# FFN down projection of two token passes by a seven-product scheme, on one core

## The chip, the core and the metric

The kernel runs on one core of a Trainium2 chip. The metric is the device time of one execution in microseconds. Engines are named as in the profile: PE is the matrix engine (PEld its weight loads), DVE the vector engine, ACT the scalar engine, POOL GpSimd, SP the engine that issues most transfers.

## What is computed

One layer of a transformer-like trunk: a gated mixer beside a cross-attention into 256 memory tokens, a projection with a normalised residual, and then a gated feed-forward network (FFN) with another normalised residual. D is 1024, there are 2048 tokens, and the FFN is 2816 wide.

```python
x = layer_norm(ALPHA * x + branch @ w_o, ln1_g, ln1_b)
x = layer_norm(ALPHA * x + swiglu_ffn(x, ffn_w_in, ffn_w_down), ln2_g, ln2_b)
# swiglu_ffn:
h = x @ w_in
(jax.nn.silu(h[..., :D_FF]) * h[..., D_FF:]) @ w_down
```

Matrices are stored transposed on the chip: features lie on the 128 partitions, tokens along the free axis. So x has 8 feature tiles, the FFN's inner width has 22 width tiles, and the output 8 output tiles.

## The kernel before

Every operand of a matmul is an fp32 matrix cut in a high and a low part (`split`, L71: ACT writes the rounded high part, L73, and DVE the rest, L74). A product of two split matrices takes three matmuls (`PASSES`: high by high, high by low, low by high).

After the mixer (to about 740 us of the span) the FFN runs in three token passes of 688, 680 and 680 tokens (`Pass`, `FPASSES`; their tiles carry the numbers 0, 1 and 2). A pass goes through its 22 width tiles in five blocks (`FBLOCKS`: 5, 4, 4, 4, 5). In a block come first the up projections (`up`, one for each width tile f), then the down projection of the block (`down`).

`up` works by seven products in place of eight already: the two halves of the tokens, the two halves of the inner dimension and the two matrices of the gate make 2x2 blocks, and the products run in the order 1, 6, 2, 5, 7, 3, 4 (12 matmuls each), into four PSUM banks. Between them DVE and ACT read the banks (`stages`). The weight combinations of products 3, 5, 6 and 7 are made in the first pass and kept in DRAM (`keep`, `ready`, L90). At the end the gated tile is split into `g`.

`down` takes each output tile m in turn: the weights of the block's nb width tiles are fetched (`weights`, tile `r_d`) and split (`w_d`), then 2 x nb x 3 matmuls of 340 tokens (344 in the first pass) fill two banks, and DVE adds each bank to the residual tile `fa` (L447 in the first block, L450 after). The fetch stands one output tile ahead of its matmuls. In the last block of a pass `done` also prepares the next pass's operands (`ffn.load`); in the last block of the third pass the columns are cut in 424 and 256.

The normalisation of a finished pass (`norm_steps`) runs between the products of the next pass's first five up projections; its last step stores `fa` (L460), and `residual` (L424) then loads the next pass's `fa` from `x1d` into the same buffers.

Tiles come from rings: raw weights `raw` has 4 buffers, split weights `wsp` 5, so that a tile waits until the one four (five) before it is read. A scheduler fixes the order of each engine's instructions when the program is built; PE keeps the order of the code. Each engine, and SP's queue, works through its own list in order, so that an instruction that waits holds up all behind it.

## Time and profile before

| | |
|---|---|
| time, median of 3 runs | 2175.59 us (2174.63 to 2178.59) |
| profiled execution: time / span | 2175.97 us / 2174.2 us |
| PE busy | 2111.3 us, 97% of the span |
| DVE busy | 1484.8 us, 68% |
| ACT busy | 874.4 us, 40% |
| POOL busy | 329.0 us, 15% |
| mean granted clock of PE | 0.993 |
| first pass, second, third (span's time) | 740 to 1231, 1231 to 1690, 1690 to 2174 us |

Busy times are of an engine's own instructions; a share is of the whole span, over stages that differ. In groups of instructions the columns are: line, engine, operation, output and inputs, shape and count, then busy time and mean duration in ns, then the idle time of the engine ahead of them and what ended it. In a timeline the columns are start, duration, instruction and count, and idle time with its releaser.

### The profile page before, as it was taken

The numbers are of one execution on the slowest core, as the hardware profiler recorded it, in microseconds if no ns is written. First come the engines' busy times: TensorE is split into PE (matmuls) and PEld (weight loads), VectorE is DVE, ScalarE is ACT, GpSimd is POOL, SyncE is SP. The second block draws the span as 40 slices with busy tenths as digits, with TensorE's granted clock in tenths as the row PEclk, the third lists the DMA queues.
The fourth block names the chain that finished last, engine by engine and source line by source line (L and its number), as shares of the span: only waits on it lengthen the run. The fifth ranks groups of instructions, "written<-read, shape, count | busy, mean of one in ns | idle before, by whom it ended". The sixth has DMA issues, their size and how long they took to land.

```text
span 2174.2 us, 34544 instructions
## 1 busy us (share of the span) xinstructions
PE 2111.3 (97%) x13130; PEld 2003.1 (92%) x13130; DVE 1484.8 (68%) x2702; ACT 874.4 (40%) x1710; POOL 329.0 (15%) x254
## 2 busy tenths in 40 slices
PE   9999999999999989999999999999999999999997
PEld 7888788788888879999999999999999999999996
DVE  7986796798789795767767874544548754454457
ACT  5553653564474452433434452222224342222234
POOL 1412321331322450000000320000002300000003
PEclk9999999999999999999999999999999999999998
DMA  6233314234333555545545565454454666445453
GB/s 214 78 110 124 117 64 160 98 107 143 129 97 111 174 201 191 208 161 178 196 158 204 192 229 194 156 194 150 160 197 147 222 220 204 154 148 198 150 181 99
DMA packets 126982, 348.83 MB, mean 160 GB/s; under 512 B 12640, under 2 KB 22880, under 8 KB 126816
## 3 DMA queue, kind: packets, MB, share of 16 engines
q1 hardware_dynamic: 113664, 299.41, 41.6%
q10 hardware_dynamic: 12672, 46.14, 5.4%
q8 instruction: 103, 1.69, 0.3%
q0 software_dynamic: 480, 1.07, 0.2%
q14 instruction: 63, 0.52, 0.1%
HBM read 283.66 MB, written 62.91 MB: 159 GB/s over the span
## 4 chain that ended last, share of the span: by engine, by line
PE 70%; DVE 17%; DMA 5%; issue 4%; ACT 3%; POOL 2%; ACTq 0%; DVEq 0%; SPq 0%; POOLq 0%
PE h L60 37%; PE d L60 19%; PE v L60 5%; PE u L60 3%; PE y L60 2%; DMA r_x<-in_xT 2%; DVE x L74 2%; DVE w_o L74 1%; DMA r_f<-x1d 1%; DVE w_u L74 1%; DVE z L567 1%; POOL s_a L233 1%; ACT p L610 1%; DVE w L74 1%; DVE w_d L74 1%
## 5 line engine op out<-in xcount | busy, mean ns | idle before, releaser
L60 PE MATMUL h<-x,w 128*128 128x340 f32 (+1 forms) x5544 | 878.6, 320 | 10.0 <-ACT m L405 3.3
L60 PEld LDWEIGHTS h<-x,w 128*128 128x128 f32 x5544 | 868.7, 188 | 16.0 <-ACT m L405 5.2
L60 PE MATMUL d<-g,w_d 128*128 128x340 f32 (+3 forms) x3168 | 504.7, 320 | 7.1 <-DVE w_d L74 4.2
L60 PEld LDWEIGHTS d<-g,w_d 128*128 128x128 f32 x3168 | 497.5, 189 | 11.4 <-DVE w_d L74 5.9
L73 ACT CAST w<-r_u 128x512 fp32r<-128x512 f32 x198 | 121.6, 619 | 260.1 <-PE h L60 163.0
L60 PE MATMUL y<-br,w_o 128*128 128x512 f32 x960 | 224.4, 395 | 0.0
L60 PEld LDWEIGHTS y<-br,w_o 128*128 128x128 f32 x960 | 180.4, 188 | 42.1
L60 PE MATMUL v<-w_v,x 128*128 128x512 f32 x768 | 187.8, 401 | 6.5 <-ACT w_v L73 4.8
L450 DVE TENSOR_TENSOR fa<-fa,d 128x340 f32<-128x340 f32 (+3 forms) x192 | 97.2, 507 | 132.4 <-PE d L60 132.4
L74 DVE TENSOR_TENSOR w<-r_u,w 128x512 fp32r<-128x512 f32 x198 | 141.1, 715 | 66.4 <-ACT w L73 56.6
L60 PEld LDWEIGHTS v<-w_v,x 128*128 128x128 f32 x768 | 143.5, 190 | 42.0 <-ACT w_v L73 4.8
L73 ACT CAST w_d<-r_d 128x512 fp32r<-128x512 f32 (+2 forms) x184 | 95.4, 521 | 202.5 <-PE d L60 145.8
L74 DVE TENSOR_TENSOR w_d<-r_d,w_d 128x512 fp32r<-128x512 f32 (+2 forms) x184 | 108.8, 597 | 48.4 <-ACT w_d L73 45.7
L369 POOL TENSOR_TENSOR t<-r_f,r_f 128x340 f32<-128x340 f32 (+1 forms) x12 | 13.9, 1161 | 813.0 <-DMA r_f<-x1d 406.4
L73 ACT CAST g<-c 128x340 fp32r<-128x340 f32 (+1 forms) x132 | 63.1, 478 | 109.7 <-DVE c L393 109.6
L60 PE MATMUL u<-xt,w_u 128*128 128x256 f32 x768 | 97.2, 282 | 0.0
L60 PEld LDWEIGHTS u<-xt,w_u 128*128 128x128 f32 x768 | 94.5, 191 | 0.0
L60 PE MATMUL u<-x,w_u 128*128 128x256 f32 x576 | 79.2, 289 | 13.1 <-DVE u L576 7.0
L60 PEld LDWEIGHTS u<-x,w_u 128*128 128x128 f32 x576 | 72.4, 192 | 16.0 <-issue 7.9
L405 DVE TENSOR_TENSOR u<-h,m 128x340 f32<-128x340 f32 (+1 forms) x66 | 33.8, 512 | 76.7 <-PE h L60 76.5
L74 DVE TENSOR_TENSOR w_o<-r_o,w_o 128x512 fp32r<-128x512 f32 (+1 forms) x96 | 69.6, 733 | 22.3 <-ACT w_o L73 22.2
L73 ACT CAST w<-s_u 128x512 fp32r<-128x512 f32 x88 | 53.0, 621 | 75.2 <-PE d L60 34.5
(185 smaller groups left out, 2384.8 us busy)
## 6 DMA issues: line engine op xcount, KB each, us to landing
w<-k_u SPq DMA_DIRECT2D x176, 512.0 KB, 4.0
r_u<-in_w SPq DMA_DIRECT2D x88, 512.0 KB, 3.3
k_u<-w ACTq DMA_DIRECT2D x88, 512.0 KB, 2.9
r_d<-in_w SPq DMA_DIRECT2D x72, 256.0 KB, 2.7
r_d<-in_w SPq DMA_DIRECT2D x56, 320.0 KB, 2.9
r_u<-in_wuq SPq DMA_DIRECT2D x32, 512.0 KB, 3.3
r_o<-in_wo SPq DMA_DIRECT2D x32, 512.0 KB, 3.4
r_v<-in_wv SPq DMA_DIRECT2D x31, 512.0 KB, 4.3
```

What stands on the lines that cost most here:

```text
L60: in_order(nc.tensor.matmul(*args, **kw))
L73: nc.scalar.copy(hi, src)
L74: engine.tensor_sub(lo, src, hi.bitcast(F32))
L233: nc.gpsimd.tensor_add(self.s2, self.s2, sq)
L369: nc.gpsimd.tensor_sub(t3, b22, b12)
L405: stages = {1: lambda: nc.scalar.copy(m1, q0), 6: lambda: nc.vector.tensor_add(u2, q1, m1), 2: lambda: nc.scalar.activation(m1, q0, AF.Sil ...
L450: nc.vector.tensor_add(y, y, p)
L567: nc.vector.tensor_scalar(z[h][:, b], z[h][:, b], mv[:, b, 0:1], rs[:, b:b + 1], ALU.subtract, ALU.mult)
L610: nc.scalar.activation(pr[:, h, :], svs[h // 2][:, h % 2, :], AF.Exp, scale=HD ** -0.5, bias=mxv[:, h:h + 1], accum_out=sm[:, h:h + 1])
```

## The change

In the second and third pass the blocks become 4, 4, 4, 4, 6. The first four blocks of these passes (16 of 22 width tiles) are projected down by `down7`; the fifth, six wide, by `down` as before. In `down7` two output tiles (a pair j, four pairs in a block), two halves of the width tiles (even and odd f) and two halves of the tokens make 2x2 blocks, and seven products of 6 matmuls each run in the order 1, 6, 2, 5, 7, 3, 4 into four banks. After every product DVE adds a bank to a quarter of `fa` or to `fu`, which holds what three quarters share and is added to them in the fourth block. Two products share a bank: 2 goes into that of 1, 3 into that of 5, 4 into that of 7, each after the add that reads the first.

`pair` makes the seven right operands `gp1` to `gp7` from two neighbouring up projections; `left` makes the left ones from the raw weights of two output tiles, in the second pass with four sums on DVE, and keeps products 5, 6 (`w5`) and 7, 3 (`w7`) in DRAM; the third pass loads these. The up projection that follows a block stands ahead of the block's `down7`, and `whole` splits the gated tiles of the plain blocks. To make room, `u4` is dropped, `tmp` has 9 buffers for 8, `g` 7 for 5, `sq` 2 for 4, `ln` 1 for 2.

```diff
 OPERANDS = (25, 3)
 NCHUNK = SEQ // TC
 FPASSES = (688, 680, 680)
-FBLOCKS = (5, 4, 4, 4, 5)
+FBLOCKS = ((5, 4, 4, 4, 5), (4, 4, 4, 4, 6), (4, 4, 4, 4, 6))
 ALPHA = 2.0 ** 0.25
 EPS = 1e-5
 
...
 
         def up(self, f, work):
             no, h = self.no, self.h
-            sums = nc.gpsimd if f < FBLOCKS[0] else nc.vector
+            sums = nc.gpsimd if f < 5 else nc.vector
             name = f"{no}_{f}"
             q0, q1, q2, q3 = banks = [bank(f"h{i}_{name}")[:, 0:h] for i in range(4)]
-            m1, u2, u4, c12, c21, c22 = (self.tmp(f"{x}_{f}") for x in ("m1", "u2", "u4", "c12", "c21", "c22"))
-            g = open_pools["g"].tile([P, 2, self.n], F32R, tag="g", name=f"g{name}")
-
-            def gate(i, x, y):
-                nc.vector.tensor_mul(y, y, x)
-                split(g[:, 0, i * h:(i + 1) * h], g[:, 1, i * h:(i + 1) * h], y)
+            m1, u2, c12, c21, c22 = (self.tmp(f"{x}_{f}") for x in ("m1", "u2", "c12", "c21", "c22"))
 
             def sum3():
                 nc.vector.tensor_add(c12, q2, u2)
...
 
             def sum4():
                 nc.vector.tensor_add(c21, q3, u2)
-                gate(1, c12, c22)
-                gate(0, m1, c21)
+                nc.vector.tensor_mul(c22, c22, c12)
+                nc.vector.tensor_mul(c21, c21, m1)
 
             stages = {1: lambda: nc.scalar.copy(m1, q0), 6: lambda: nc.vector.tensor_add(u2, q1, m1),
-                      2: lambda: nc.scalar.activation(m1, q0, AF.Silu), 5: lambda: nc.vector.tensor_add(u4, q2, u2),
-                      7: lambda: nc.vector.tensor_add(c22, q3, u4), 3: sum3, 4: sum4}
+                      2: lambda: nc.scalar.activation(m1, q0, AF.Silu), 5: lambda: nc.vector.tensor_add(c22, q2, u2),
+                      7: lambda: nc.vector.tensor_add(c22, q3, c22), 3: sum3, 4: sum4}
 
             def then(stage):
                 def run():
...
             left = plain(*wab) if no else halves(*wab, sums, False)
             products(left, lambda p, k, b: self.x[p][k][:, b], banks,
                      name, {p: then(stage) for p, stage in stages.items()}, (1, 6, 2, 5, 7, 3, 4), 0, key=f"u{f}")
+            return c21, c22
+        def whole(self, f, ys):
+            g = open_pools["g"].tile([P, 2, self.n], F32R, tag="g", name=f"g{self.no}_{f}")
+            for i in (1, 0):
+                split(g[:, 0, i * self.h:(i + 1) * self.h], g[:, 1, i * self.h:(i + 1) * self.h], ys[i])
             return g
+        def pair(self, i, blk, even, odd):
+            if i == 0:
+                self.gp = {p: open_pools["g"].tile([P, 2, 2, self.h], F32R, tag="g", name=f"gp{self.no}_{blk}_{p}")
+                           for p in range(1, 8)}
+            (b11, b12), (b21, b22) = even, odd
+            def put(p, src):
+                split(self.gp[p][:, i, 0], self.gp[p][:, i, 1], src)
+            put(1, b11)
+            put(2, b21)
+            put(3, b22)
+            nc.vector.tensor_sub(b11, b12, b11)
+            put(5, b11)
+            nc.vector.tensor_sub(b12, b22, b12)
+            nc.vector.tensor_sub(b22, b22, b11)
+            put(6, b22)
+            put(7, b12)
+            nc.vector.tensor_sub(b21, b21, b22)
+            put(4, b21)
+        def left(self, blk, m, f0, q):
+            name, key, half = f"e{self.no}_{blk}_{m}", f"e{blk}_{m}", 2 * q * P
+            r = raw([P, 2, 2 * q, P], f"r_{name}")
+            for a in range(2):
+                nc.sync.dma_start(out=r[:, a], in_=w2[m + a, :, f0:f0 + 2 * q, :])
+            v = r.rearrange("p a (i j) x -> p a j i x", j=2)
+            a11, a12, a21, a22 = (v[:, a, j] for a in range(2) for j in range(2))
+            made = f"{key}_5" not in kept
+            if made:
+                s = raw([P, 4, q, P], f"r_s{name}")
+                nc.vector.tensor_add(s[:, 0], a21, a22)
+                nc.vector.tensor_sub(s[:, 1], s[:, 0], a11)
+                nc.vector.tensor_sub(s[:, 2], a11, a21)
+                nc.vector.tensor_sub(s[:, 3], a12, s[:, 1])
+            out = {}
+            t = wsp([P, 2, 2, q, P], f"w1_{name}")
+            for j in range(2):
+                split(t[:, j, 0], t[:, j, 1], v[:, 0, j])
+                out[j + 1] = t[:, j]
+            def sums(n):
+                pa, pb = ((5, 6), (7, 3))[n]
+                if made:
+                    t = wsp([P, 2, 2, q, P], f"w{pa}_{name}")
+                    split(t[:, :, 0], t[:, :, 1], s[:, 2 * n:2 * n + 2])
+                    keep(f"{key}_{pa}", t)
+                else:
+                    t = ready(f"{key}_{pa}", f"{pa}_{name}")
+                out[pa], out[pb] = t[:, 0], t[:, 1]
+            sums(0)
+            sums(1)
+            t = out[4] = wsp([P, 2, q, P], f"w4_{name}")
+            split(t[:, 0], t[:, 1], a22)
+            return out
+        def down7(self, blk, q, f0, last):
+            h, n, gp = self.h, self.n, self.gp
+            if blk == 0:
+                self.u = [open_pools["sums"].tile([P, 4, P], F32, tag="sums", name=f"fu{self.no}_{m}")
+                          .rearrange("p a b -> p (a b)")[:, 0:h] for m in range(0, KD, 2)]
+            w = [self.left(blk, 0, f0, q)]
+            for j in range(KD // 2):
+                if j < KD // 2 - 1:
+                    w.append(self.left(blk, 2 * j + 2, f0, q))
+                y, u, wj = self.out[j], self.u[j], w[j]
+                c11, c12, c21, c22 = (y[:, a, b * h:(b + 1) * h] for a in range(2) for b in range(2))
+                q0, q1, q2, q3 = (bank(f"e{i}_{self.no}_{blk}_{j}")[:, 0:h] for i in range(4))
+                to = {1: (q0, True, False), 6: (q1, True, True), 2: (q0, False, True), 5: (q2, True, False),
+                      7: (q3, True, False), 3: (q2, False, True), 4: (q3, False, True)}
+                def add(y, p, first=False):
+                    if first and blk == 0:
+                        nc.vector.scalar_tensor_tensor(out=y, in0=y, scalar=ALPHA, in1=p, op0=ALU.mult, op1=ALU.add)
+                    else:
+                        nc.vector.tensor_add(y, y, p)
+                for p in (1, 6, 2, 5, 7, 3, 4):
+                    bk, start, stop = to[p]
+                    for i in range(q):
+                        for x, (a, b) in enumerate(PASSES):
+                            matmul(bk, wj[p][:, a, i, :], gp[p][:, i, b], start=start and i == 0 and x == 0,
+                                   stop=stop and i == q - 1 and x == 2, skip_group_check=True)
+                    if p == 1:
+                        if blk == 0:
+                            nc.scalar.copy(u, q0)
+                        else:
+                            add(u, q0)
+                    elif p == 6:
+                        add(u, q1)
+                    else:
+                        add(*{2: (c11, q0, True), 5: (c22, q2, True), 7: (c22, q3), 3: (c12, q2, True),
+                              4: (c21, q3, True)}[p])
+                if last:
+                    nc.vector.tensor_add(c12, c12, u)
+                    nc.vector.tensor_tensor(out=y[:, 1].rearrange("p (b t) -> p b t", b=2),
+                                            in0=y[:, 1].rearrange("p (b t) -> p b t", b=2),
+                                            in1=u.unsqueeze(1).broadcast_to([P, 2, h]), op=ALU.add)
 
         def residual(self):
             for m in range(0, KD, 2):
...
 
         if (j, m) == (0, 1):
             close("x", "sums", "xt", "mixer")
-            pool("tmp", 8)
+            pool("tmp", 9)
             pool("sums", 4)
             pool("operands0", OPERANDS[0])
             ffn.load(0)
...
 
     close("big", "y")
     pool("operands1", OPERANDS[1])
-    pool("ln", 2, "right")
+    pool("ln", 1, "right")
     pool("acc", KD // 2, "right")
-    pool("g", 5, "right")
-    pool("sq", 4, "right")
+    pool("g", 7, "right")
+    pool("sq", 2, "right")
     late.norm.squares = open_pools["sq"]
     ffn.rest()
     work = norm_steps([late.norm], [late.store], 5, 5)
...
         pa, h, n = ffn, FPASSES[no] // 2, FPASSES[no]
         whole = (((h, n), (0, h)),)
         f0 = 0
-        for blk, nb in enumerate(FBLOCKS):
-            gs = [pa.up(f, work) for f in range(f0, f0 + nb)]
+        blocks = FBLOCKS[no]
+        ahead = []
+        def up(f):
+            return f, pa.up(f, work)
+        for blk, nb in enumerate(blocks):
+            end = blk == len(blocks) - 1
+            fs = range(f0 + len(ahead), f0 + nb)
+            if no and not end:
+                ys = list(ahead)
+                for f in fs:
+                    ys.append(up(f))
+                    if len(ys) % 2 == 0:
+                        pa.pair(len(ys) // 2 - 1, blk, ys[-2][1], ys[-1][1])
+                ahead = [up(f0 + nb)]
+            else:
+                gs = [pa.whole(*y) for y in ahead] + [pa.whole(*up(f)) for f in fs]
+                ahead = []
             if blk == 0:
                 for _ in work:
                     pass
                 pa.residual()
-            if blk < len(FBLOCKS) - 1:
+            if no and not end:
+                pa.down7(blk, nb // 2, f0, blk == len(blocks) - 2)
+            elif not end:
                 pa.down(blk, gs, f0, whole, lambda ci, m: None)
             elif no < len(FPASSES) - 1:
                 ffn = Pass(no + 1)
```

Three places show how the lists of DVE and SP stand now. In tile names the first number after the letters is the pass (`e0_1_2_0`: bank 0, pass number 1, block number 2, pair 0; `c22_12_1`: width tile 12 of pass 1).

DVE at the start of the third block of the second pass, before: the last gate of width tile 12, and then the adds of the first output tiles.

```order
L393 TENSOR_TENSOR c22_12_1_14741<-c22_12_1_14741,c12_12_1_14739 128x340
L401 TENSOR_TENSOR c21_12_1_14740<-h3_1_12_14735,u2_12_1_14737 128x340
L74 TENSOR_TENSOR g1_12_14742<-c22_12_1_14741,g1_12_14742 128x340
L393 TENSOR_TENSOR c21_12_1_14740<-c21_12_1_14740,m1_12_1_14736 128x340
L74 TENSOR_TENSOR w_d1_2_4_0_0_14968<-r_d1_2_4_0_14966,w_d1_2_4_0_0_14968 128x512
L74 TENSOR_TENSOR g1_12_14742<-c21_12_1_14740,g1_12_14742 128x340
L450 TENSOR_TENSOR fa1_0_13214<-fa1_0_13214,d1_2_0_340_14872 128x340
L450 TENSOR_TENSOR fa1_0_13214<-fa1_0_13214,d1_2_0_0_14886 128x340
L74 TENSOR_TENSOR w_d1_2_5_0_0_15001<-r_d1_2_5_0_14999,w_d1_2_5_0_0_15001 128x512
```

DVE there now:

```order
L392 TENSOR_TENSOR c12_12_1_14809<-h2_1_12_14805,u2_12_1_14808 128x340
L74 TENSOR_TENSOR w4_e1_2_0_14950<-r_e1_2_0_14927,w4_e1_2_0_14950 128x256
L396 TENSOR_TENSOR c21_12_1_14810<-h3_1_12_14806,u2_12_1_14808 128x340
L398 TENSOR_TENSOR c21_12_1_14810<-c21_12_1_14810,m1_12_1_14807 128x340
L397 TENSOR_TENSOR c22_12_1_14811<-c22_12_1_14811,c12_12_1_14809 128x340
L74 TENSOR_TENSOR w1_e1_2_2_14961<-r_e1_2_2_14953,w1_e1_2_2_14961 128x256 x2
L502 TENSOR_TENSOR fu1_0_13213<-fu1_0_13213,e0_1_2_0_14979 128x340
L456 TENSOR_TENSOR r_se1_2_4_15035<-r_e1_2_4_15032 128x256
L502 TENSOR_TENSOR fu1_0_13213<-fu1_0_13213,e1_1_2_0_14980 128x340
L457 TENSOR_TENSOR r_se1_2_4_15035<-r_se1_2_4_15035,r_e1_2_4_15032 128x256
L502 TENSOR_TENSOR fa1_0_13205<-fa1_0_13205,e0_1_2_0_14979 128x340
```

Each pair has seven adds in place of four, each reading a bank that PE needs again, and between them stand the sums and splits of the next pairs' weights; two gate products and the split of `w1` of the second pair stand ahead of the first add.

DVE some rows on in that block, before (second to fourth output tile), and then now (second pair):

```order
L450 TENSOR_TENSOR fa1_0_13214<-fa1_0_13214,d1_2_1_340_14905 128x340
L450 TENSOR_TENSOR fa1_0_13214<-fa1_0_13214,d1_2_1_0_14919 128x340
L74 TENSOR_TENSOR w_d1_2_6_0_0_15034<-r_d1_2_6_0_15032,w_d1_2_6_0_0_15034 128x512
L450 TENSOR_TENSOR fa1_2_13216<-fa1_2_13216,d1_2_2_340_14938 128x340
L450 TENSOR_TENSOR fa1_2_13216<-fa1_2_13216,d1_2_2_0_14952 128x340
L74 TENSOR_TENSOR w_d1_2_7_0_0_15067<-r_d1_2_7_0_15065,w_d1_2_7_0_0_15067 128x512
L450 TENSOR_TENSOR fa1_2_13216<-fa1_2_13216,d1_2_3_340_14971 128x340
```

```order
L502 TENSOR_TENSOR fu1_2_13214<-fu1_2_13214,e0_1_2_1_15058 128x340
L74 TENSOR_TENSOR w4_e1_2_2_14976<-r_e1_2_2_14953,w4_e1_2_2_14976 128x256
L74 TENSOR_TENSOR w1_e1_2_4_15040<-r_e1_2_4_15032,w1_e1_2_4_15040 128x256 x2
L502 TENSOR_TENSOR fu1_2_13214<-fu1_2_13214,e1_1_2_1_15059 128x340
L502 TENSOR_TENSOR fa1_2_13207<-fa1_2_13207,e0_1_2_1_15058 128x340
L456 TENSOR_TENSOR r_se1_2_6_15114<-r_e1_2_6_15111 128x256
L74 TENSOR_TENSOR w5_e1_2_4_15045<-r_se1_2_4_15035,w5_e1_2_4_15045 128x2x256
L502 TENSOR_TENSOR fa1_2_13207<-fa1_2_13207,e2_1_2_1_15060 128x340
L74 TENSOR_TENSOR w7_e1_2_4_15050<-r_se1_2_4_15035,w7_e1_2_4_15050 128x2x256
```

Where one split stood between two adds before, now the first sum of the fourth pair (L456, from the raw tile `r_e1_2_6`) stands ahead of the adds of products 5 to 4 of the second pair. That raw tile lies in the buffer of `r_e1_2_2`, which `w4_e1_2_2`, four rows up from L456, reads last.

SP in the first block of the third pass, where the second pass's output is stored and the residual loaded, before, and then now:

```order
L460 DMA out_T<-fa1_0_13214 128x2x340
L460 DMA out_T<-fa1_2_13216 128x2x340
L460 DMA out_T<-fa1_4_13218 128x2x340
L424 DMA fa2_0_17848<-x1d_82 128x2x680
L460 DMA out_T<-fa1_6_13220 128x2x340
L424 DMA fa2_2_17850<-x1d_82 128x2x680
L424 DMA fa2_4_17852<-x1d_82 128x2x680
L424 DMA fa2_6_17854<-x1d_82 128x2x680
L104 DMA r_d2_0_4_0_17990<-in_w2 128x640
```

```order
L90 DMA w_5_e2_0_0_18125<-k_e0_0_5_13233 128x1024
L565 DMA out_T<-fa1_6_13211 128x2x340
L565 DMA out_T<-fa1_0_13205 128x2x340
L565 DMA out_T<-fa1_2_13207 128x2x340
L565 DMA out_T<-fa1_4_13209 128x2x340
L565 DMA out_T<-fa1_6_13211 128x2x340
L529 DMA fa2_0_18105<-x1d_82 128x2x680
L529 DMA fa2_2_18107<-x1d_82 128x2x680
L529 DMA fa2_4_18109<-x1d_82 128x2x680
L529 DMA fa2_6_18111<-x1d_82 128x2x680
L90 DMA w_7_e2_0_0_18127<-k_e0_0_7_13238 128x1024
L90 DMA w_5_e2_0_2_18140<-k_e0_2_5_13259 128x1024
```

Before, raw weights of the fifth output tile stood behind the loads of `fa`. Now the kept weights of products 7 and 3 of the very first pair, `w_7_e2_0_0`, stand behind all four of them.

More of the change, by code (lines that the diff above doesn't have):

```diff
@@ L200, in tile @@
         def tile(self, tag, pool=common):
-            return pool.tile([P, 512], F32, tag=tag, name=f"{tag}_{self.name}")[:, 0:self.n]
+            return pool.tile([P, 512 if pool is common else 432], F32, tag=tag, name=f"{tag}_{self.name}")[:, 0:self.n]
         def add(self, y):
@@ L454, in norm @@
             norm = Norm("l2g", "l2b", tb - ta, f"b{self.no}_{ta}",
-                        pairs=[y[:, :, ta:tb] for y in self.out] if pairs else None, sums=open_pools["ln"])
+                        pairs=[y[:, :, ta:tb] for y in self.out] if pairs else None, sums=open_pools["ln"] if pairs or ta else None)
             norm.squares = open_pools["sq"]
```

## The prediction

> **What bounds the kernel now.** I read the busy times first, then the two changed passes as windows, then the groups with each shape apart, and at last the timelines of single places. Page of the profile:
>
> ```profile
> span 2174.2 us, 34544 instructions
> ...
> PE 2111.3 (97%) x13130; PEld 2003.1 (92%) x13130; DVE 1484.8 (68%) x2702; ACT 874.4 (40%) x1710; POOL 329.0 (15%) x254
> ```
>
> The profiled execution took 2175.97 us, 1.8 more than its span and 0.4 above the median of the runs. The second pass as one window:
>
> ```profile
> 1231.00:1690.00 459.00, 457.03 (x2930) 455.19 (x2929) 257.02 (x499) 144.81 (x292) 34.32 (x33) 1.00 0.55 183
> ```
>
> PE works 457.03 of 459 us at a clock of 1.00; DVE (third value) 257.02, or 56%. The pass lasts as long as its matmuls, so a matmul less is a gain only as long as nobody makes PE wait. PE stood still just twice there, at the pass's end:
>
> ```profile
> 1680.86 4.96 PE L60 MATMUL d<-g,w_d 128*128 128x340 f32 x30 [0.74 <-DVE w_d L74]
> 1686.93 1.36 PE L60 MATMUL d<-g,w_d 128*128 128x340 f32 x7 [1.11 <-DVE w_d L74]
> ```
>
> The shapes that the sum needs:
>
> ```profile
> L60 PE MATMUL d<-g,w_d 128*128 128x340 f32 x1872 | 294.0, 318 | 2.0 <-DVE w_d L74 1.9
> L450 DVE TENSOR_TENSOR fa<-fa,d 128x340 f32<-128x340 f32 x112 | 56.7, 507 | 94.1 <-PE d L60 94.1
> L60 PE MATMUL d<-g,w_d 128*128 128x424 f32 x120 | 23.7, 357 | 0.2 <-DVE g L74 0.2
> L60 PE MATMUL d<-g,w_d 128*128 128x256 f32 x120 | 17.4, 294 | 0.2
> L520 DVE TENSOR_TENSOR s<-r_x,s 128x256 f32<-128x256 f32 x32 | 13.4, 417 | 0.0
> ```
>
> A matmul's own duration is 318 ns, but they overlap: 294.0 / 1872 = 157.05 ns is what one costs PE. The same holds for DVE:
>
> ```profile
> 1752.35 1.76 DVE L280 TENSOR_TENSOR fa<-fa,rstd_b 128x340 f32<-128x340 f32 x4
> ...
> 909.49 1.28 DVE L74 TENSOR_TENSOR w<-r_u,w 128x512 fp32r<-128x512 f32 x2
> 910.69 0.68 DVE L74 TENSOR_TENSOR w<-s_u,w 128x512 fp32r<-128x512 f32 x1
> ```
>
> Four of 340 elements in 1.76 us, the last about 0.50 long: (1.76 - 0.50) / 3 = 0.42 apart. Two of 512: (910.69 - 909.49) / 2 = 0.60 apart. Both are some 0.08 under their durations, so 256 elements (417 ns) cost 0.33.
>
> **The change part by part.**
>
> *Matmuls.* 16 width tiles took 16 x 8 outputs x 2 halves x 3 = 768 matmuls in a pass; four blocks of four pairs of 42 make 672. In two passes 192 go: 192 x 157.05 ns = **-30.2 us**.
>
> *The plain block.* It is six wide in place of five, at the same matmuls for each width tile. The third pass cuts its columns in 424 and 256 there: (23.7 + 17.4) / 120 - 2 x 0.15705 = 0.028 us dearer for each pair of matmuls, 24 pairs more: **+0.7**. An output tile of the second pass gets 36 matmuls for its split weights in place of 30, 0.9 us more, so I let the waits of 0.74 and 1.11 go: **-1.9** (other bound 0).
>
> *Room on DVE in a pair.* 42 matmuls take 6.6 us, a product 0.94. In the second pass DVE has, for each pair, seven adds (2.9), three splits of 256 (w1 twice, w4: 1.0), four sums of 256 (1.3) and two splits of 512 (w5, w7: 1.2): 6.4 us, 97% of PE's time, where it had four adds and two splits. In the third, without sums and with w5 and w7 loaded, 4.0. Hand-overs:
>
> ```profile
> 1221.31 0.55 DVE L74 TENSOR_TENSOR w_d<-r_d,w_d 128x384 fp32r<-128x384 f32 x1
> 1221.91 1.37 PE L60 MATMUL d<-g,w_d 128*128 128x344 f32 x7 [1.26 <-DVE w_d L74]
> ...
> 1231.54 4.68 PE L60 MATMUL h<-x,w 128*128 128x340 f32 x29
> ...
> 1235.55 0.51 DVE L405 TENSOR_TENSOR u<-h,m 128x340 f32<-128x340 f32 x1 [3.29 <-PE h L60]
> ```
>
> DVE to PE: 1221.91 - 1221.86 = 0.05. PE to DVE: 24 matmuls end at 1231.54 + 3.77 = 1235.31, DVE starts 0.24 later. An add therefore frees its bank 0.24 + 0.50 + 0.05 = 0.8 after the product, against 0.94 until the next product ends: product 2 needs the bank of 1, 3 that of 5, 4 that of 7, each one product later. About 0.15 of slack beyond an undelayed add; whatever DVE does ahead of it is a wait of PE, as long as DVE has no idle time to recover in, which in the second pass it hasn't.
>
> *Start of a block.* By the first piece of DVE's list, add c21, two gate products (dependent, 0.54 and 0.42) and two w1 splits (0.66) stand between the last product of the up projection and the first add: 0.24 + 0.55 + 0.54 + 0.42 + 0.66 + 0.5 = 2.9 until the bank is free; PE is there after two products, 1.88: **0.95** a block.
>
> *Second pair.* Its list has L456 ahead of the add of product 5. The raw tile r_e6 of L456 can be fetched only after w4 of the second pair (some 2.0 us into it), in two transfers:
>
> ```profile
> r_d<-in_w SPq DMA_DIRECT2D x72, 256.0 KB, 2.7
> ```
>
> Landed at 2.0 + 2.7 + 0.5 for the second issue = 5.2; L456, the w5 split and the add finish at 6.65, where product 3 needs the bank at 4.7: **2.0** a block. Were the buffer free a product earlier, 1.0; were the transfer as slow as the 7.4 below, 6.7.
>
> *Rest of a block*: small slips at products 3 and 4 from DVE's 97%, **0.75**. So the second and third block of the second pass wait 3.7 each. In the fourth, the shared part is added at each pair's end (0.42 and, for 680 elements, 680/512 x 0.60 = 0.8: 1.2 us), on a DVE with 0.15 to spare: 3.7 + 3 x 1.05 = 6.9. In the first the w4 split stands behind twelve L280 (1.25), the first pair waits 1.35, the second 2.5 (its raw load stands behind the residual's loads on SP), then 0.2: 5.3. Together 5.3 + 3.7 + 3.7 + 6.9 = **19.6**.
>
> *Third pass, first block.* Kept weights w_7_e2_0_0 stand on SP behind stores and residual loads. Before, there:
>
> ```profile
> 1751.79 7.92 PE L60 MATMUL h<-x,w 128*128 128x340 f32 x48
> 1759.55 15.73 PE L60 MATMUL d<-g,w_d 128*128 128x340 f32 x100
> ...
> 1760.41 5.57 SPq L424 DMA_DIRECT2D fa<-x1d  x3
> 1766.04 1.43 SPq L104 DMA_DIRECT2D r_d<-in_w  x3
> ...
> DMA to landing us min/median/max: 3.0/4.0/6.3
> ...
> DMA to landing us min/median/max: 6.8/7.4/7.8
> ```
>
> The third row lets the transfer behind the loads go at 1766.0. The fifth row is of kept weights (L90, whole run), the last of the raw loads just here. So w7 lands at 1770 to 1773.5, while PE needs it four products (3.8) after the block's start (1759.6 + 1.25): 1764.6. I take **6** (5.4 to 9), and 1.25 for the w4 split. Here DVE has room: blocks two and three 0.5 each; the fourth 0.5 and, from pair to pair, the add of 1.2 us ahead of the next first add, 0.67 x 3: 2.5. Together **10.8**.
>
> *Hidden work.* `pair` adds three splits and four subtractions per two width tiles (3 us of DVE in 26 us of up projections, where it idles 44%); ACT has three casts more there. Kept weights add 32 x 512 KB = 17 MB written, then read: 37 GB/s beside 183. Without that cover they'd cost up to 8 x 2 x 3 = 48 us; a DVE with 200 us idle excludes most of it.
>
> *Clock.* Waits of 2 us are not only their own length:
>
> ```profile
> 814.17 4.13 PE L60 MATMUL h<-x,w 128*128 128x344 f32 x13 [1.93 <-ACT w L73]
> ...
> 837.01 1.30 PE L60 MATMUL d<-g,w_d 128*128 128x344 f32 x4 [1.90 <-ACT g L73]
> ...
> 86.69 2.17 PE L60 MATMUL u<-x,w_u 128*128 128x256 f32 x12 [1.98 <-DVE u L576]
> ...
> 781.28 2.92 PE L60 MATMUL h<-x,w 128*128 128x344 f32 x17 [1.86 <-DVE u L406]
> ```
>
> ```profile
> 814.00:818.00 4.00, 3.70 (x13) 3.40 (x14) 2.98 (x3) 1.78 (x4) 1.60 (x1) 0.58 1.11 285
> 838.00:842.00 4.00, 4.00 (x17) 4.00 (x17) 1.78 (x4) 0.96 (x2) 0.00 (x0) 0.57 0.15 35
> 84.00:90.00 6.00, 4.03 (x26) 3.85 (x25) 6.00 (x9) 2.43 (x5) 2.95 (x2) 0.80 0.53 174
> 765.00:790.00 25.00, 20.64 (x131) 19.81 (x130) 24.34 (x33) 12.60 (x25) 18.10 (x13) 1.00 0.45 168
> ```
>
> After three of four gaps of 1.86 to 1.98 us the granted clock (third value from the end) fell to 0.57 or so for 4 us: 4 x 0.42 = 1.7 us each. Five waits of 2 us and more (one in each block of the second pass, w7 in the third): 5 x 1.7 x 3/4 = **+6.4** (0 to 14).
>
> The Trainium skill, TensorE: Matmul & The Clock Gate, section HAM oscillation, asks for "no PE-idle gaps >~3.4µs"; by that only w7's wait would count, 1.7 in place of 6.4. The clock row after 814.17 speaks against it: 1.93 us were enough.
>
> *Sum*: -30.2 + 0.7 - 1.9 + 19.6 + 10.8 + 6.4 = +5.4 on 2176.0: **2181.4**. The waits, 30.4, are the soft term: between 10 (w7 and four block starts alone) and 48 (the raw transfer of r_e6 landing in 7.4 in place of 2.7 in each of four blocks, 4 x 4.7 more).
>
> **Rivals.** *Half the waits, faster*: DVE was idle 44% of the pass and PE waited for it 2 us in all; if it gets to sums and splits early enough that adds stand first, about 15 us remain, with one fall of the clock: 2176.0 - 31.4 + 15 + 1.7 = 2161.3. Against it: the list is in order, and rows ahead of an add can't be passed. It decides where waits and clock together stay under 27.
>
> *No change*: waits as priced, but the clock falls only after w7's: 2181.4 - 4.7 = 2176.7. For it: the 1.86 us gap at 781.28, clock 1.00 around it. That is also what the page's rule gives.
>
> *Kept weights late in the third pass, slower still*: a pair's w5 takes (ring of five) the buffer in which the pair before has its w1, read last by product 2, 2.9 us into that pair; landing takes 4.0 to 6.3, so it is there at 6.9 to 9.2, where product 6 needs it at 6.6 + 0.94 = 7.5. At the median nothing, at the slowest 1.6 x 12 pairs = 19: 2200. For it the 6.8 to 7.8 seen in the first block; against it the median.
>
> **Chances.** Forecast 0.32 (its own range 2176 to 2190), faster 0.30, no change 0.20, slower still 0.18. The range takes in the faster case's 15 give or take 4 and the slower one to its price: 2157 to 2200. A measurement of this kernel tells 0.2% (4.4 us) from no change; faster by more 0.30, within 0.24 (the no-change case and the forecast's lower end), slower 0.46.
>
> **What would show it.** In the trace after: 1344 matmuls of the new banks e; idle time of PE ahead of them released by DVE's L502, most in the second pair and the fourth block of the second pass; DVE waiting at L456 for r_e6; a wait near 6 us in the third pass's first block that ends with w_7; clock rows under 0.9 in windows behind these. The forecast is wrong if PE waits under 25 us in both passes, if DVE's share in a block of `down7` is well under 90%, or if the clock stays at 1.00.

## The result

The changed kernel took 2206.94 us (median; 2202.70 to 2207.44), the kernel before 2177.09 in the same runs: ratio 1.0129, 95% interval 1.0105 to 1.0153. The profiled execution's span is 2205.7 against 2174.2 us, 31.5 more. Slower was the likeliest sign in the prediction, but the time was put at 2181.4 and the range ended at 2200. The page after, and the second and third pass as windows (a window's row has the stretch, its length, the busy time of PE, PEld, DVE, ACT and POOL with counts, then the granted clock, the share of DMA and GB/s):

```profile
span 2205.7 us, 34775 instructions
...
PE 2103.8 (95%) x12938; PEld 1982.4 (90%) x12938; DVE 1613.8 (73%) x3030; ACT 909.8 (41%) x1814; POOL 330.6 (15%) x254
```

```profile
1236.00:1711.00 475.00, 452.73 (x2829) 442.40 (x2829) 339.74 (x710) 171.73 (x360) 35.91 (x34) 0.99 0.62 213
1712.00:2205.00 493.00, 460.91 (x2876) 451.38 (x2875) 306.70 (x643) 162.68 (x340) 34.73 (x31) 0.97 0.60 205
```

PE lost 192 instructions (13130 to 12938), as it should, yet the second pass takes 475.7 us in place of 458.9 and the third, to the end, 494.2 in place of 483.7 (from the starts of their first up projections). In the second pass DVE is now busy for 340 us instead of 257. The groups of the banks e (new products) and d (plain blocks); L502 is DVE's add of a bank, L500 the first add of a quarter in the first block, L512 ACT's copy of product 1's bank there:

```profile
L60 PE MATMUL e<-gp,w_e 128*128 128x340 f32 x1344 | 227.7, 326 | 31.1 <-DMA w_e<-k_e 9.4 <-DVE fu L502 8.8 <-DVE fa L502 8.4
...
L60 PE MATMUL d<-g,w_d 128*128 128x340 f32 x288 | 45.4, 318 | 0.5 <-DVE g L74 0.5
```

The 1344 matmuls of the new products should cost 1344 x 157 ns = 211 us. They were busy for 227.7 (the slow clock, and short stalls inside the pipeline, are in there) and PE idled 31.1 ahead of them. In what follows the *excess* of a group of matmuls is the sum, over them, of the time from one matmul's start to the next one's on PE, less 0.157 us each; waits and slow clock are both in it. For the up projections it is given as the difference to the kernel before.

| place | predicted | excess measured |
|---|---|---|
| second pass, block 1 / 2 / 3 / 4 | 5.3 / 3.7 / 3.7 / 6.9 | 11.1 / 4.3 / 4.2 / 7.6 |
| third pass, block 1 / 2 / 3 / 4 | 7.25 / 0.5 / 0.5 / 2.5 | 12.1 / 1.7 / 1.3 / 4.3 |
| clock | 6.4 | in these rows and the next |
| up projections of the two passes | 0 | 12.0 |
| ahead of the second pass | 0 | 4.3 |

The new products' rows add to 46.5; -30.2 + 0.7 - 1.9 + 46.5 + 12.0 + 4.3 = 31.4, the difference of the spans to 0.1. The 0.7 and -1.9 in it are the predicted terms. Counted as excess, the second pass's last block lost 2.0 and the end of the third 1.1, while the plain blocks that went had stood 1.9 below 0.157 us a matmul: together -1.2 too, so that the sum closes partly by luck. Of the 4.3 ahead of the second pass, 2.7 stand already at the start of the FFN's first up projection (753.2 for 750.5 us). That start lies between 750.4 and 754.2 us in the other profiles; a cause is not shown.

Places on PE's timeline, in this order: an up projection beside the normalisation, the first block of the second pass (two rows), its second block (two rows), the first block of the third:

```profile
1271.62 5.86 PE L60 MATMUL h<-x,w 128*128 128x340 f32 x36 [2.42 <-ACT m L400]
...
1320.04 7.41 PE L60 MATMUL e<-gp,w_e 128*128 128x340 f32 x36 [2.94 <-DVE fa L502]
1330.74 17.12 PE L60 MATMUL e<-gp,w_e 128*128 128x340 f32 x96 [3.29 <-DVE fa L500]
...
1402.91 10.12 PE L60 MATMUL e<-gp,w_e 128*128 128x340 f32 x60 [0.79 <-DVE fu L502]
1414.61 14.85 PE L60 MATMUL e<-gp,w_e 128*128 128x340 f32 x90 [1.58 <-DVE fa L502]
...
1800.33 25.53 PE L60 MATMUL e<-gp,w_e 128*128 128x340 f32 x144 [9.18 <-DMA w_e<-k_e]
```

The second block reads as priced: idle for 0.79 at its start and 1.58 at the second pair, 0.94 and 2.28 lost from matmul to matmul (0.95 and 2.0 priced). The first blocks do not. In the second pass ACT and with it DVE stood still there (two rows of ACT, then DVE's, then SP's):

```profile
1318.22 0.62 ACT L73 CAST w_e<-r_se 128x512 fp32r<-128x512 f32 x1 [4.02 <-DMA k_e<-w_e]
1325.23 0.71 ACT L73 CAST w_e<-r_e 128x256 fp32r<-128x256 f32 x2 [1.96 <-DMA r_e<-in_w]
...
1318.87 0.69 DVE L74 TENSOR_TENSOR w_e<-r_se,w_e 128x512 fp32r<-128x512 f32 x1 [3.05 <-ACT w_e L73]
...
1314.51 5.93 SPq L450 DMA_DIRECT2D r_e<-in_w  x4
```

ACT's cast of the second pair's w7 goes into the ring buffer of the first pair's w5, and that buffer is still being *read* by the store of kept weights (`keep`, L83). Behind that cast on ACT, and behind its subtraction on DVE, stand the adds. I had counted PE as the only reader of these buffers. That is the wait of 2.94. Ahead of the wait of 3.29, at the second pair, ACT waited 1.96 for raw weights, whose transfers stand on SP behind the residual's (last row), as the prediction had read.

In the third pass the order of SP's queue was as read (residual loads, then w7), but the transfers were slower than any row of before showed:

```profile
1787.06 4.44 SPq L529 DMA_DIRECT2D fa<-x1d  x4
1791.55 2.15 SPq L90 DMA_DIRECT2D w_e<-k_e  x3
...
DMA to landing us min/median/max: 3.1/4.3/9.8
```

The wait was 9.18 us, where 6 (5.4 to 9) stood in the sum. The w7 transfer, the first of the three in the second row, was issued 4.3 us after the block's start, earlier than priced (5.2), but landed some 8.7 later. The last row is of L90 in the third pass: up to 9.8 us, against 6.3 before.

The granted clock in windows behind the waits of 2.94 (two rows), 3.29, 2.38 (on ACT's copy, in the third pass) and 9.18 us (two rows), and then behind the waits of 2.42, 1.58 and 1.78 us:

```profile
1320.00:1324.00 4.00, 3.96 (x17) 3.96 (x18) 1.25 (x3) 0.85 (x2) 0.00 (x0) 0.67 1.04 407
1324.00:1328.00 4.00, 3.45 (x20) 3.17 (x19) 1.97 (x6) 1.07 (x3) 0.00 (x0) 0.91 0.53 209
1332.00:1336.00 4.00, 4.00 (x19) 4.00 (x18) 2.71 (x7) 1.56 (x4) 0.00 (x0) 0.63 0.80 308
1748.00:1752.00 4.00, 4.00 (x18) 4.00 (x17) 3.45 (x10) 2.11 (x5) 0.00 (x0) 0.57 0.04 16
1800.00:1804.00 4.00, 3.67 (x13) 3.68 (x14) 0.51 (x1) 0.00 (x0) 0.00 (x0) 0.50 1.01 391
1804.00:1808.00 4.00, 4.00 (x22) 4.00 (x21) 2.13 (x6) 1.56 (x4) 0.00 (x0) 0.75 0.26 91
...
1272.00:1276.00 4.00, 4.00 (x28) 4.00 (x27) 4.00 (x13) 2.38 (x6) 0.00 (x0) 1.00 0.02 6
1416.00:1420.00 4.00, 4.00 (x28) 4.00 (x27) 3.68 (x10) 1.25 (x4) 0.00 (x0) 1.00 0.90 301
1584.00:1588.00 4.00, 2.94 (x20) 2.67 (x19) 3.80 (x9) 0.72 (x3) 0.00 (x0) 1.00 0.89 298
```

Behind the first wait 4 x 0.33 + 4 x 0.09 = 1.7 us are lost; behind the second 4 x 0.37 = 1.5, and 0.2 in the window before it (0.95); behind the third 1.7. Behind 9.18 it is 3.7 x 0.5 + 4 x 0.25 = 2.8. Together nearly 8, against 6.4 predicted, but at other places: it was priced as one spell of slow clock in each block of the second pass (taken three times in four) and one behind w7. Two came in the first block, none in the other three, and one in an up projection.

### The profile page after: what moved, and what is told of

It is laid out like the page before. It is cut to its first block, busy times and chain, and to the rows that moved or that the text cites. A ratio compares the mean times of both kernels' runs of the same rounds, so it can differ in the third digit from the quotient of the medians.

```text
span 2205.7 us, 34775 instructions
## 1 busy us (share of the span) xinstructions
PE 2103.8 (95%) x12938; PEld 1982.4 (90%) x12938; DVE 1613.8 (73%) x3030; ACT 909.8 (41%) x1814; POOL 330.6 (15%) x254
## 4 chain that ended last, share of the span: by engine, by line
PE 63%; DVE 18%; DMA 8%; ACT 5%; issue 4%; POOL 2%; SPq 0%; ACTq 0%; DVEq 0%; POOLq 0%
PE h L60 35%; PE d L60 9%; PE e L60 7%; PE v L60 5%; PE u L60 3%; DMA r_x<-in_xT 2%; DVE w_o L74 1%; DVE w_u L74 1%; DVE w L74 1%; DMA r_f<-x1d 1%; DMA r_e<-in_w 1%; DVE x L74 1%; PE y L60 1%; POOL s_a L233 1%; ACT p L715 1%
## 5 line engine op out<-in xcount | busy, mean ns | idle before, releaser
L60 PE MATMUL h<-x,w 128*128 128x340 f32 (+1 forms) x5544 | 884.3, 320 | 18.9 <-ACT m L400 8.7
L60 PEld LDWEIGHTS h<-x,w 128*128 128x128 f32 x5544 | 872.3, 189 | 26.4 <-ACT m L400 9.9
L60 PE MATMUL d<-g,w_d 128*128 128x344 f32 (+3 forms) x1632 | 262.7, 321 | 4.8 <-DVE w_d L74 2.0
L60 PEld LDWEIGHTS d<-g,w_d 128*128 128x128 f32 x1632 | 257.9, 189 | 7.8 <-DVE w_d L74 2.6
L60 PE MATMUL e<-gp,w_e 128*128 128x340 f32 x1344 | 227.7, 326 | 31.1 <-DMA w_e<-k_e 9.4
L60 PEld LDWEIGHTS e<-gp,w_e 128*128 128x128 f32 x1344 | 214.6, 192 | 43.1 <-DVE fa L502 11.2
L73 ACT CAST w_d<-r_d 128x384 fp32r<-128x384 f32 (+2 forms) x104 | 53.5, 520 | 92.3 <-PE d L60 66.2
L502 DVE TENSOR_TENSOR fa<-fa,e 128x340 f32<-128x340 f32 x128 | 64.6, 506 | 36.5 <-PE e L60 35.4
L73 ACT CAST w_e<-r_e 128x256 fp32r<-128x256 f32 x96 | 35.9, 404 | 132.5 <-PE e L60 101.4
```

Source lines behind the costliest of these rows:

```text
L60: in_order(nc.tensor.matmul(*args, **kw))
L73: nc.scalar.copy(hi, src)
L502: nc.vector.tensor_add(y, y, p)
```

## The experiments

Ratios are to the kernel before in the same runs; excess as above, of the new products in the second and third pass; pass lengths from the profiled execution. The changed kernel's row stands first. A difference of two ratios carries some 6 us, both intervals taken together. The profile of the kernel before is of 2176 us, and beside the experiments that kernel took 2180 to 2181, so that lengths set against its profile carry some 5 us over the whole span.

| run | median us | ratio (95% interval) | excess, 2nd / 3rd | 2nd / 3rd pass |
|---|---|---|---|---|
| (changed) | 2206.94 | 1.0129 (1.0105 to 1.0153) | 27.1 / 19.4 | 475.7 / 494.2 |
| before_sq2 | 2187.28 | 1.0030 (1.0019 to 1.0041) | none | 462.8 / 486.6 |
| after_sq4 | 2199.86 | 1.0083 (1.0065 to 1.0101) | 32.4 / 20.0 | 478.4 / 491.0 |
| pool_sums | 2209.00 | 1.0127 (1.0109 to 1.0146) | 23.8 / 19.8 | 474.8 / 494.2 |
| order_p2 | 2196.90 | 1.0071 (1.0056 to 1.0086) | 13.5 / 18.9 | 467.0 / 491.9 |
| kept_early | 2203.36 | 1.0101 (1.0084 to 1.0117) | 27.5 / 14.0 | 477.8 / 486.8 |
| no_keep | 2200.15 | 1.0092 (1.0073 to 1.0111) | 18.5 / 20.4 | 468.4 / 493.2 |
| combined | 2191.97 | 1.0053 (1.0038 to 1.0068) | 11.9 / 14.5 | 464.2 / 488.7 |
| combined_norm | 2180.70 | 1.0003 (0.9994 to 1.0013) | 12.5 / 13.1 | 459.4 / 482.8 |
| no_keep_all | 2174.94 | 0.9973 (0.9962 to 0.9983) | 10.9 / 12.2 | 455.3 / 482.3 |
| spread | 2155.42 | 0.9883 (0.9867 to 0.9899) | 3.5 / 3.4 | 447.4 / 472.1 |

**The buffers given up: before_sq2 and after_sq4.** What made the up projections wait, whose matmuls the diff does not touch? ACT's timeline of the changed kernel shows squares of the normalisation waiting for POOL, and the copy of product 1's bank behind them:

```profile
1266.25 0.49 ACT L229 ACTIVATE sq_b<-fa 128x344 f32<-128x344 f32 x1 [0.84 <-POOL s_b L233]
...
1271.13 0.43 ACT L400 COPY m<-h 128x340 f32<-128x340 f32 x1
```

```diff
 # before_sq2, on the kernel before
-    pool("sq", 4, "right")
+    pool("sq", 2, "right")
 # after_sq4, on the changed kernel (square_tile): two of `sq`, two of the common pool, in turn
-            if self.squares is None:
+            self.turn = not self.turn
+            if self.squares is None or self.turn:
```

> The kernel before with one number changed: two buffers for squares in place of four, as the changed kernel has. Theory: the changed kernel's up projections of width tiles 1 and 2 lose 3.7 us in the second pass and 3.6 in the third, without the clock, because ACT's squares wait for POOL to free one of two buffers and the copy of product 1's bank stands behind them on ACT. Then this kernel loses nearly the same: 5 to 9 us, 2182 to 2186, with ACT's squares waiting for POOL and PE waiting for the copy m. Rival: that loss comes from the extra splits and subtractions of the right operands in the same place; then this kernel stays within 1.5 us of the kernel before.

Measured 0.30% (6.5 us): within the theory. The answer for the squares in the second pass, of who waits for whom, has

```profile
  POOL s_b L233: 3.8, 7
```

seven waits of squares for POOL, where the kernel before has none there. The second pass grew by 3.9 us, the third by 2.9, the first by 2.4.

> The changed kernel with squares in four buffers again (two of its own pool and two of the common one, in turn). Theory: as measured on the kernel before, two buffers cost 6.5 us, and the up projections of width tiles 1 and 2 lose 7.3 us with it in the later passes; four give back 5 to 9 us: 2198 to 2202. Rival: in the changed kernel the extra splits of the right operands keep ACT and DVE late at that place anyway: under 2 us, 2205 to 2209.

Four buffers bring the ratio from 1.0129 to 1.0083, about 10 us with an interval of some 6; in the profiled execution the up projections of the two passes lose 5.7 us instead of 12.0, while the new products' excess happens to be 6 larger: the waits of the second pass's third and fourth block were 1.95 and 2.47 us there, and behind both the granted clock fell to 0.50. So the loss in the up projections is mostly the squares; what is left is the w4 split at the end of width tile 4 (1.2 in each pass, which the prediction had put into the first blocks) and 1.6 at tile 2. The exact size is not settled better than 4 to 10 us.

**DVE's load or DVE's order: pool_sums and order_p2.**

```diff
 # pool_sums: the four sums in left()
-                nc.vector.tensor_add(s[:, 0], a21, a22)
+                nc.gpsimd.tensor_add(s[:, 0], a21, a22)
...
 # order_p2: down7
-                for p in (1, 6, 2, 5, 7, 3, 4):
+                for p in ((1, 6, 5, 7, 2, 3, 4) if self.no == 1 else (1, 6, 2, 5, 7, 3, 4)):
```

> The changed kernel with the four sums of every pair's weights in the second pass on POOL in place of DVE. Theory: DVE's list is what PE waits for in the second pass (the sums stand ahead of adds, and the first of them waits for a transfer): the waits at the second pair (1.7 to 3.4 us) and in the fourth block go, the excess of the e matmuls in that pass falls from 27 us to 8 to 14, and the time to 2188 to 2196. Rival: the raw transfer itself is late, or POOL at about 0.9 us a sum is late with what the splits need; then the waits stay where they are with POOL as the cause, and the time is 2203 to 2212.

No gain, a miss. The second pairs' waits in blocks 2 and 3 did vanish (1.58 and 1.55 us of idle PE, none here), so L456 ahead of the adds was the cause there; but these are the small ones. The first block became 11.9, with a wait of 5.78 us (PE's row, then ACT's):

```profile
1334.08 11.21 PE L60 MATMUL e<-gp,w_e 128*128 128x340 f32 x53 [5.78 <-DVE fa L500]
...
1329.08 0.71 ACT L73 CAST w_e<-r_e 128x256 fp32r<-128x256 f32 x2 [4.01 <-DMA r_e<-in_w]
```

Now the raw weights, behind the residual loads on SP, came last.

> The changed kernel with the products of the second pass in the order 1, 6, 5, 7, 2, 3, 4, so that an add has two to four products until its bank is needed again instead of one or two. Theory: waits come from adds that are late by one to two us on a DVE that has, over a pair, just enough time; the block starts (0.95 each) and the second pairs' waits shrink, by 8 to 12 us together: 2195 to 2199. Rival: DVE is the bound of a pair (6.4 of 6.6 us), and the waits come back one product later: 2204 to 2209.

12.6 us less by the ratios, just past what was expected; the profiled second pass is 8.7 shorter. DVE has the same instructions in each pair; only the distance from an add to the next use of its bank has grown. Blocks 2 and 3 of the second pass fell from 4.3 and 4.2 to 0.3 and 0.5 us, the fourth from 7.6 to 2.7. DVE as the bound of a pair is out: 97% was no bound, the slack of 0.15 us was. The rival was right in a part, though: some 3.4 us came back in the up projections behind the first three blocks, which now wait for their own kept weights, 0.9 to 1.0 us each (the up projections' group in the changed kernel, then here):

```profile
L60 PE MATMUL h<-x,w 128*128 128x340 f32 x3696 | 585.7, 319 | 8.5 <-ACT m L400 4.8 <-DVE w L74 1.8 <-DVE c L401 1.7
...
L60 PE MATMUL h<-x,w 128*128 128x340 f32 x3696 | 586.2, 320 | 11.3 <-ACT m L400 4.8 <-DMA w<-k_u 2.9 <-DVE w L74 1.8
```

The first block kept 10.1 of its 11.1 us: PE waited 5.0 us there for ACT's copy of product 1's bank, behind the cast that waits for the store (6.2 here).

**The kept weights: kept_early and no_keep.**

```diff
 # kept_early: the third pass's first left() ahead of the residual
+            w0 = pa.left(blk, 0, f0, nb // 2) if no == 2 and blk == 0 else None
             if blk == 0:
...
                 pa.residual()
 # no_keep: both passes make the sums
-            made = f"{key}_5" not in kept
+            made = True
...
-                    keep(f"{key}_{pa}", t)
```

> The changed kernel with the kept weights of products 7 and 3 of the third pass's first pair issued ahead of the four residual loads (which go later by one issue). Theory: the 9.3 us wait in that block is the place of this transfer in SP's list: it is issued 4.5 us earlier, the wait falls to 3 to 5 us (the residual loads then end it), with less of the slow clock behind it: 2200 to 2203. Rival: the transfers are at their limit there (DMA share 1.0), so that whichever is issued first the last needed one lands at the same time: 2205 to 2208.

About 6 us less by the ratios, no more than their noise; the third pass is 7.4 shorter in the profile. The wait of 9.2 became two, 1.0 for w7 and then 2.5 for the residual, the next in line:

```profile
1792.82 1.22 PE L60 MATMUL e<-gp,w_e 128*128 128x340 f32 x6 [1.00 <-DMA w_e<-k_e]
1796.49 8.77 PE L60 MATMUL e<-gp,w_e 128*128 128x340 f32 x37 [2.46 <-DVE fa L500]
```

> The changed kernel without the kept weights of the down projection: the third pass makes its four sums and splits on DVE as the second does, nothing is written to or read from DRAM for them. Theory: in the second pass's first block ACT's cast into a ring buffer waits 4.0 us until the store of kept weights out of that buffer has landed, and in the third pass's first block PE waits 9.3 us for the load; both go. The first block of the second pass falls from 11.1 us of excess to 3 to 6, the third pass's blocks come to what the second pass's are now (4 to 8 each, against 12.1, 1.7, 1.3, 4.3), and the time is 2195 to 2203. Rival: the residual loads alone hold up that place (the adds need them); then the first blocks keep 9 us or more, the later blocks of the third pass get dearer, and the time is 2207 to 2215.

8 us less: the first block of the second pass 4.9 in place of 11.1, so the stores were the larger part of it. The run takes away their traffic too; that they hold a buffer is shown by ACT's wait of 4.02 us. The third pass's first block kept 8.9 (its second pair now waits, 4.19 us and slow clock), a miss of that part.

**Together: combined and combined_norm.** `combined` has order_p2, kept_early and the closing adds on POOL; `combined_norm` has also three narrower square buffers and

```diff
-                work = norm_steps(norms, [pa.store(0, h), pa.store(h, n)], 6, 0)
+                work = norm_steps(norms, [pa.store(0, h), pa.store(h, n)], 3, 0)
```

> Three edits on the changed kernel together: the second pass's products in the order 1, 6, 5, 7, 2, 3, 4; the kept weights of the third pass's first pair ahead of the residual loads; the two closing adds of the fourth block on POOL. If the waits are separate, the gains add: 12.6 us and 6 us as measured alone, and 3 to 6 for the closing adds (0.5 to 1.5 us at each pair of the fourth block, in both passes): 2182 to 2187 where the changed kernel takes 2207 and the kernel before 2177. Rival: the waits only move (an add that comes in time lets PE run into the next late transfer), the gains add to less than 15 us: above 2191.

0.76% under the changed kernel, some 17 us where 20 to 25 were expected; the closing adds on POOL gave nothing (fourth block of the third pass 4.6 for 4.3).

> The kernel called combined, and in it three buffers for squares, each just wide enough, in place of two, and the normalisation's steps beginning three products earlier. Theory: the squares cost 2.4 us and their clock in each pass, and the residual loads and kept weights of a first block come late because the normalisation ends late: 5.6 us earlier stores, 2 to 4 us less at the squares, 4 to 8 less in the first blocks: 6 to 12 us under combined. Rival: an earlier normalisation takes DVE and ACT from the up projections' own bank reads while POOL still adds the last sums, and PE waits there instead: within 3 us of combined, or above it.

11 us under `combined`, and level with the kernel before: with the excess nearly as it was (25.6 for 26.4), the gain is in the up projections (15.8 to 5.4 us; 2.2 of the 5.4 stand right behind matmuls of the normalisation, from whose starts they are counted).

**What was left: no_keep_all and spread.**

> The kernel called combined_norm without kept weights: both passes make their own, in the order 1, 6, 5, 7, 2, 3, 4. If DVE's order and the kept weights' transfers were the causes, e matmuls keep under 6 us of excess in each pass and the time is 2160 to 2172, below the kernel before. Rival: on a DVE with 6.4 us of work in 6.6 us a pair, and the first block's residual loads, 8 us or more stay in each pass: 2174 to 2184, no gain on the kernel before.

0.27% faster than before: the time is at the border of theory and rival, and the excess of 10.9 and 12.2 us is what the rival said. The second and third blocks of both passes are at zero, the fourth at 3.5 us; both first blocks wait at their second pair (7.8 and 9.2):

```profile
1319.91 0.43 DVE L456 TENSOR_TENSOR r_se<-r_e 128x256 f32<-128x256 f32 x1 [2.28 <-DMA r_e<-in_w]
```

Their raw weights stand behind the residual. The 3.5 us of the fourth blocks go with POOL's closing adds (below). `spread` takes both away:

```diff
+            w0 = [pa.left(blk, m, f0, nb // 2) for m in (0, 2)] if no and blk == 0 else None
...
                 pa.residual()
...
 # closing adds on DVE, one pair after each of the next up projections
-            return f, pa.up(f, work)
+            ys = pa.up(f, work)
+            pa.close_pair()
+            return f, ys
```

(and four square buffers, as in after_sq4).

> The kernel called no_keep_all with three edits: squares in four buffers; the raw weights of a first block's second pair loaded ahead of the residual instead of behind it; the closing adds of the fourth block on DVE again, one pair after each of the next up projections, in place of POOL at each pair. Theory: what is left there are three places with one cause each: the second pair's raw load (3.9 and 5.2 us, each with a spell of slow clock, 8 and 9 us of excess), POOL's closing adds during which DVE's 256-element sum took 1.88 us in place of 0.42 (3.5 us in each pass), and the squares in the first pass (about 3). Without them the e matmuls keep under 3 us of excess in each pass and the time is 2148 to 2158. Rival: the loads at that place share one queue and one limit, so that the residual comes later by what the raw weights come earlier, and the adds wait for it: over 5 us of excess stay in each first block, 2164 to 2172.

The time is as expected, 1.17% under the kernel before; 3.5 and 3.4 us of excess are left where under 3 was expected. Its page, second pass and group e:

```profile
span 2154.4 us, 34761 instructions
...
1235.00:1682.00 447.00, 443.40 (x2831) 441.67 (x2830) 339.77 (x710) 171.83 (x360) 36.63 (x35) 1.00 0.56 189
...
L60 PE MATMUL e<-gp,w_e 128*128 128x340 f32 x1344 | 214.5, 320 | 4.7 <-DVE fa L501 3.9 <-DVE fa L503 0.8
```

DVE is as busy as in the changed kernel (339.77 for 339.74 us) in a pass 28 us shorter. Against the kernel before, the two passes are 23.1 us shorter: -30.2 + 0.7 - 1.9 + 6.9 of excess + 1.8 in the up projections (nearly all of it right behind matmuls of the normalisation) = -22.7, to 0.4 us. The first pass is still 3.5 longer.

## Why the prediction was wrong

- **Matmuls, -30.2: right.** 192 fewer instructions, and `spread`, in which little waits, gets the gain.
- **DVE's lateness in the blocks without a special neighbour: right in mechanism and nearly in size.** The second pass's blocks 2 to 4 were priced 14.3 and took 16.0; the third pass's blocks 2 to 4, 3.5 and 7.3, since each block start costs 0.6 and each closing pair 1.1 where 0.5 for the whole block and 0.67 stood. The sentence that DVE's 97% leaves no room to recover was the wrong reason: with the same load and another order of products most of the waits went.
- **First blocks: mis-sized.** Priced 12.6 us with the w4 splits and without clock; measured 23.2 and 2.4 for the w4 splits (which fell in up projections), of which 6.2 are slow clock: 19.4 in place of 12.6. Two steps failed. The stores of kept weights were counted as traffic only ("hidden work", 37 GB/s), not as readers that hold a ring buffer and with it ACT's list. And the landing of w7 was taken from rows of a place that was loaded for a shorter time: the DMA share stood at 1.04 and 0.97 from 1764 to 1772 us before, at 0.90 to 1.04 from 1788 to 1804 in the changed kernel.
- **The buffers given up: no term at all.** The change says that `sq` goes from 4 to 2, and the prediction priced everything else; it cost about 6.5 us by itself, through POOL, ACT and the banks of up projections whose matmuls were not changed. Of the 12.0 us in the up projections 2.4 are the w4 splits and 1.7 slow clock; 7.9 had no term.
- **Clock: right in kind, in its total by luck.** 6.4 predicted, nearly 8 seen, and a spell costs the 1.7 us that was read from the kernel before. The waits that were to bring it (1.58 to 1.78 us in the second pass's blocks 2 to 4) brought none; the first block brought two spells for one, w7's lasted longer, and one came in an up projection. By the limit of 3.4 us that the Trainium skill gives (TensorE: Matmul & The Clock Gate, HAM oscillation) only the wait of 9.18 would have counted; the rows after 2.94, 3.29 and 2.38 us are against it.
- **The miss as a sum.** 31.5 measured less 5.4 predicted is 26.1 us: 6.9 of waits in the first blocks, 5.5 in the other new blocks, 7.9 in the up projections, 1.5 of clock, and 4.3 ahead of the second pass, whose cause stays open.
- **Slips of arithmetic.** The start of a block, 2.9 less 1.88, is 1.0 and not 0.95, and the upper bound of the waits, 30.4 + 4 x 4.7, is 49 and not 48; neither matters.
- **Rivals.** "Kept weights late in the third pass" happened in the first pair, and beside it once with 0.25 us. "No change" and "half the waits" failed on the first blocks and the squares. The range ended at the dearest single rival; no case joined a dearer first block with a term that was missing.

## What to carry to other kernels

With in-order engines, price the *slack* of each result (the time until its bank or buffer is wanted again), not only the engine's share: giving each add two to four products in place of one or two, with not an instruction less, was worth 12.6 us by the ratios and 8.7 in the profiled second pass. Every pool that a change makes smaller to find room is an edit of its own with a price, and every DMA that reads a ring buffer is one of its readers. When a wait is taken away, ask which transfer of the same queue comes next: kept weights, raw weights and residual took turns here until most had been moved.

## What the hardware showed beside that

POOL's closing adds stopped DVE. In `no_keep_all` (DVE's rows, then POOL's):

```profile
1570.27 1.88 DVE L458 TENSOR_TENSOR r_se<-r_e 128x256 f32<-128x256 f32 x1
1572.06 0.41 DVE L459 TENSOR_TENSOR r_se<-r_e,r_se 128x256 f32<-128x256 f32 x1
...
1570.02 1.84 POOL L521 TENSOR_TENSOR fa<-fa,fu 128x680 f32<-128x680 f32 x1
```

A sum of two SBUF tiles that takes 0.42 us took 1.88 and ended 0.3 after POOL's instruction; a DVE add from PSUM beside POOL, at 1569.20, kept its 0.50. The Trainium skill, SBUF — State Buffer, section Who interferes with whom, says that a DVE instruction with two SBUF inputs contends with a GpSimd instruction that reads SBUF, because the second input comes through the read interface that the two engines share; the trace agrees.
